# Four raw weight blocks, eight split pairs and two T2 tiles in place of 12 KB of DMA scratch

## The chip, the cores and the metric

The kernel runs on one NeuronCore of a Trainium2 chip. Its engines work side by side, each with a queue of its own: TensorE (PE; its weight loads are shown as PEld), VectorE (DVE), ScalarE (ACT), GpSimd (POOL) and SyncE (SP), which only issues DMAs. The metric is the device time of one execution in microseconds; the time of a kernel is the median of its runs.

## The reference

One layer of a bidirectional encoder on 1024 tokens of width 1024, in float32. Cut to what matters:

```python
x = x + 0.5 * rms_norm(swiglu(rms_norm(x, g1a), w1_in, w1_out), g1b)     # d_ff 2816
u = rms_norm(x, gma)
rq, rk, rv, rg, nq, nk, nv, g_ret, g_na = split(u @ w_mix_in)
y = bidirectional_retention(rotary(rq), rotary(rk) * 128 ** -0.5, rv)     # 4 heads, chunks of 128
y_ret = (silu(rg) * head_norm(y)) @ w_ret_out
y_na = neighbourhood_attention(nq, nk, nv, rel_bias) @ w_na_out           # 16 x 64 grid, 8 heads
x = x + rms_norm((sigmoid(g_ret) * y_ret + sigmoid(g_na) * y_na) @ w_out, gmb)
x = x + 0.5 * rms_norm(swiglu(rms_norm(x, g2a), w2_in, w2_out), g2b)
```

Every `@` is a matrix product of float32 numbers.

## The kernel before

A product of two float32 matrices is made of three matmuls. Each operand is split into a high part h (ScalarE rounds it to fp32r, L61) and a low part l (VectorE subtracts h from it, L62; in a few places GpSimd does), and TensorE adds up a_h·b_h, a_h·b_l and a_l·b_h in one bank (`mm3`, L88 to L90). So each block of weights that TensorE uses goes through a chain: a DMA from DRAM into a raw tile `wraw` of 128 x 1024 (`raw`, L70 to L73, issued by SyncE at L72), a cast and a subtraction for each half of 512 columns into a pair `wh`, `wl` (`piece`, L75 to L80), and then 12 or 24 matmuls. These tiles lie in one pool for the whole kernel, in rings: three of `wraw`, seven of `wh`, seven of `wl`. A load waits until a split has read the tile's last use; a split waits until TensorE has used the pair.

The two input products of the FFNs and most of the mix projection use Strassen's scheme in Winograd's form: seven products instead of eight. `Pairs.run` (L494 to L536) handles one pair of weight columns as a unit: it loads two raw blocks g and u (L498), and VectorE makes t1 = b12 - b11 (L510), t2 = b22 - t1 (L511), t3 = b22 - b12 (L521) and t4 = b21 - t2 (L530); t1, t3 and t4 overwrite the raw blocks, t2 has a tile of its own (L502), one for the kernel, called `t` in the profile. Each of them is split and multiplied (`product`), and VectorE adds the results up (L517 to L535). Two of VectorE's instructions, L510 and L521, are placed behind the result addition at L524 of the unit before (`behind`, L488). The first units of each such stage start early: their first two products are made ahead (`lead`, L454) and only the other five remain for `run`.

`ffn_in` runs 22 such units; its tile `gt`, one of three, takes the results (ScalarE's copy at L509 is the first write). `LeftFactors` (L562 to L607) makes operands of the output product from them and lets GpSimd store them to DRAM (`store`, L68), 14 stores of 256 KB for each two units. `ffn_out` (L674) reads them back block by block (L625). In its epilogue rows 4 to 7 of the residual come through `raw` (L699) as well, are added to the result (L659), stored (L660), normalised (L670) and transposed by TensorE (`flip`, L127), whereupon `Winograd.put` (L271 to L298) splits them and their sums. While this goes on, the first products of the mix stage, with weights loaded by `load_w` (L82), fill TensorE. The mix stage then runs 14 units of `Pairs`, the neighbourhood attention (`na_cores`, its K loaded as `kraw` at L879), the retention and the output products; `out_proj` (L104) takes weights by `load_w` and activations through `graw` (L850), both split in the same way, for three groups of token tiles.

What sets the order: each engine runs its queue in order, and the queues are fixed when the program is built. The Tile framework's planner takes the program's order as priority and dispatches, in a run that it simulates, what has its inputs and a free buffer; `high_priority`, `behind` and `issue_after` bend that. So the number of buffers enters twice: on the chip, where an instruction waits for a tile to come free, and when the queues are made. SyncE's queue carries the loads of `wraw` together with all others, so whatever stands behind a load that waits for a buffer waits too.

GpSimd issues its own DMAs in software, and the framework reserves a scratch for them in on-chip memory, 16 KB of each partition unless told otherwise. It is shared by all stores of `store`.

Of the kernel before, what the change touches and what calls it, by code (L numbers as in the profile page):

```python
# [10 lines left out]
F32 = mybir.dt.float32  # L11
F32R = mybir.dt.float32r
# [6 lines left out]
P = 128  # L19
D = 1024  # L20
# [18 lines left out]
class Core:  # L39
# [28 lines left out]
        self.nc.gpsimd.dma_start(dst, src)  # L68

    def raw(self, src, n=D):  # L70
        raw = self.wpool.tile([P, D], F32, tag="wraw", name="wraw", bufs=3)
        self.nc.sync.dma_start(raw[:, :n], src)  # L72
        return raw  # L73

    def piece(self, src, eng=None):  # L75

        h = self.wpool.tile([P, 512], F32R, tag="wh", name="wh", bufs=7)
        l = self.wpool.tile([P, 512], F32R, tag="wl", name="wl", bufs=7)
        self.split(h, l, src, eng=eng)
        return h, l  # L80

# [327 lines left out]
class Pairs:  # L409
# [84 lines left out]
    def run(self, i, out, done):  # L494

        c, nc = self.c, self.c.nc
        tt = nc.vector.tensor_tensor
        g, u = (c.raw(a) for a in self.srcs[i])  # L498
        b11, b21, b12, b22 = g[:, :512], g[:, 512:], u[:, :512], u[:, 512:]

        t1, t3, t4 = b11, b12, b21
        t2 = c.wpool.tile([P, 512], F32, tag="t2", name="t2", bufs=1)  # L502

        begun = self.begun.get(i)
        p1 = begun[0] if begun else self.product("a11", b11)
        c11, c12 = out(0), out(2)
        u1 = c12 if begun else c11
        for p, s in self.pieces(p1):
            nc.scalar.copy(u1[:, s], p)  # L509
        self.behind(tt(t1, b12, b11, ALU.subtract))  # L510
        tt(t2, b22, t1, ALU.subtract)  # L511
        p6 = self.product("s2", t2)
        if not begun:
            tt(c12, p6, c11, ALU.add)
        p2 = begun[1] if begun else self.product("a12", b21)
        for p, s in self.pieces(p2):
            tt(c11[:, s], p, u1[:, s], ALU.add)  # L517
        done(0)
        if begun:
            tt(c12, p6, c12, ALU.add)  # L520
        self.behind(tt(t3, b22, b12, ALU.subtract))  # L521
        p7 = self.product("s3", t3)
        c21 = out(1)
        self.last = tt(c21, p7, c12, ALU.add).ins  # L524
        p5 = self.product("s1", t1)
        c22 = out(3)
        tt(c22, p5, c21, ALU.add)
        tt(c12, p5, c12, ALU.add)
        done(3)
        tt(t4, b21, t2, ALU.subtract)  # L530
        p4 = self.product("a22", t4)
        tt(c21, p4, c21, ALU.add)
        done(1)
        p3 = self.product("s4", b22)
        self.end = tt(c12, p3, c12, ALU.add).ins  # L535
        done(2)  # L536
# [499 lines left out]
def ret_cores(c, pool, spool, d, dec, fill, n):  # L1036
# [12 lines left out]
    def split_qk(raw):  # L1049
        ops = {q: [pool.tile([P, S], F32R, tag=f"{q}{p}", name=f"{q}{p}", bufs=1) for p in "hl"] for q in "kq"}  # L1050
        for b in range(2):
            bs = slice(b * 512, (b + 1) * 512)
            for q in "kq":
                c.split(*[o[:, bs] for o in ops[q]], raw[q][:, bs])
        return ops
# [83 lines left out]
    for h in range(RH):  # L1139
# [4 lines left out]
        for cc in range(NC - 1, 0, -1):  # L1144
            update(h, 1, kb, cc, vget(cc), sb[:, cc] if cc < NC - 1 else None, sb[:, cc - 1])
            fill(n[2])
            if left and cc < NC - 1:
                store(*left.pop(0))
            if cc == NC - 2:
                ops = split_qk(raw)  # L1150
# [43 lines left out]
def trunk_layer(ctx: ExitStack, tc, x, xt, g1a, w1i, w1o, g1b, gma, wmt, wnv, wrv, logits, dtab, rope, bias,  # L1194
# [133 lines left out]
    with tc.tile_pool(name="pa", bufs=1, reuse_waits="tile") as pa:  # L1328
# [12 lines left out]
        for i, (_, _, f, g, fn) in enumerate(jobs):  # L1341
            parts = {}

            def part(j):
                parts[j] = half()
                return parts[j]

            def done(j):
                h = j % 2
                if fn == "rotary":  # L1350
                    rotate(turners[j], half(), parts[j], *tabs[h])
                elif fn is not None:
                    nc.scalar.activation(parts[j], parts[j], fn)
                c.store((f, g)[j // 2][:, h * 512:(h + 1) * 512], parts[j])
            mx.run(i, part, done)
            if i == 2:
                x1pool = pool(x1_stack, "x1b", "right")
                a21[:] = [x1pool.tile([P, 4, 512], F32R, name=f"a21{q}") for q in "hl"]
                for k in range(2):
                    raw = c.raw(d["a21"][:, 2 * k:2 * k + 2].rearrange("p k t -> p (k t)"))  # L1360
                    c.split(*[q[:, 2 * k:2 * k + 2].rearrange("p k t -> p (k t)") for q in a21], raw)
            if i == NHP - 1:
                for _ in vproj(wnv, ((4, 5, 6, 7),), done_nv):
                    pass
                for cb in range(4):
                    nc.sync.dma_start(d["nvg"][cb].rearrange("t (r c) d -> (t r) c d", r=4),
                                      d["nv"][:, KEY_OFF[cb]:KEY_OFF[cb] + 32, :])
# [216 lines left out]
```

## Time and profile before

| | |
|---|---|
| median of 3 runs | 2311.84 us (2311.79 to 2312.2) |
| the profiled execution | 2309.61 us, of which its span 2307.8 us |
| TensorE busy | 2215.0 us (96%), 10232 matmuls |
| VectorE busy | 1685.7 us (73%) |
| ScalarE busy | 1001.5 us (43%) |
| GpSimd busy | 647.0 us (28%) |
| mean granted clock of TensorE | 0.991 |
| moved by DMA | 444.11 MB, 192 GB/s over the span |
| loads of `wraw` from DRAM | 218 of 512 KB, 4.2 us from issue to landing (median) |

In a timeline row of the profile the columns are the start and the length in us, the engine ("SPq" is SyncE's queue, issuing a DMA), the line of the kernel, the operation, what it writes and reads, the shapes and how many like it follow each other; in square brackets stands how long the engine was idle before it, and what ended the wait. "A <- B: t, n, m" in the table of waits means that A waited for B for t us in all, n times, m us at most.

### The profile page before, as it was taken

How to read it: one execution, taken by the hardware profiler on the slowest of the kernel's cores; microseconds unless marked ns; L12 is line 12 of the kernel's file. 1: busy time of each engine (PE TensorE's matmuls, PEld its weight loads, DVE VectorE, ACT ScalarE, POOL GpSimd, SP SyncE). 2: the span in 40 equal slices, each digit the busy share in tenths (PEclk: the TensorE clock that was granted, in tenths of full speed). 3: DMA queues.
4: the chain of work that ended last, by engine and by line, in shares of the span. 5: the costliest groups of instructions: out<-in, count | busy, mean ns of one | idle time of the engine just before them, and what ended most of it. 6: DMA issues, size and time to landing. Idle time of an engine off the chain costs nothing.

```text
span 2307.8 us, 30216 instructions
## 1 busy us (share of the span) xinstructions
PE 2215.0 (96%) x10232; PEld 1828.7 (79%) x10232; DVE 1685.7 (73%) x2928; ACT 1001.5 (43%) x2086; POOL 647.0 (28%) x779
## 2 busy tenths in 40 slices
PE   7889999999998999999999999999799999999997
PEld 5678888888776877777888888787578888888886
DVE  7888888755558668869875678546999888885443
ACT  5433434332334222248885675315544343433232
POOL 1121212168424134411101222101431212215942
PEclk9999999999999999999999999999999999999999
DMA  6345434597545542357654466766534444349864
GB/s 237 132 143 181 169 132 174 184 381 291 202 150 173 178 164 96 109 189 234 219 177 153 164 224 228 281 210 206 168 137 163 159 159 167 141 151 367 304 232 164
DMA packets 150090, 444.11 MB, mean 192 GB/s; under 512 B 18800, under 2 KB 46576, under 8 KB 147824
## 3 DMA queue, kind: packets, MB, share of 16 engines
q1 hardware_dynamic: 111216, 314.23, 40.3%
q0 software_dynamic: 38720, 127.96, 14.4%
q8 instruction: 81, 1.33, 0.2%
q14 instruction: 73, 0.60, 0.1%
HBM read 305.80 MB, written 140.51 MB: 193 GB/s over the span
## 4 chain that ended last, share of the span: by engine, by line
PE 76%; DVE 11%; issue 5%; POOL 3%; DMA 3%; ACT 2%; SPq 0%; POOLq 0%; DVEq 0%; ACTq 0%
PE ps L90 23%; PE ps L88 23%; PE ps L89 23%; DVE wl L62 2%; PE pt L88 1%; PE pt L89 1%; PE pt L90 1%; DMA wraw<-in_dram 1%; PE pt L928 1%; POOL rstd L98 1%; PE ps L909 1%; DVE t L511 0%; ACT wh L61 0%; POOL cmb L294 0%; DVE wraw L521 0%
## 5 line engine op out<-in xcount | busy, mean ns | idle before, releaser
L62 DVE TENSOR_TENSOR wl<-wraw,wh 128x512 fp32r<-128x512 f32 x512 | 365.9, 732 | 81.7 <-ACT wh L61 80.5
L61 ACT CAST wh<-wraw 128x512 fp32r<-128x512 f32 x516 | 300.9, 618 | 219.1 <-DVE wraw L530 67.8
L89 PE MATMUL ps<-wl,g 128*128 128x512 f32 x484 | 188.7, 390 | 0.0
L90 PE MATMUL ps<-wh,g 128*128 128x512 f32 x484 | 188.4, 389 | 0.0
L88 PE MATMUL ps<-wh,g 128*128 128x512 f32 x484 | 188.3, 390 | 0.0
L552 ACT ACTIVATE c<-c 128x512 f32<-128x512 f32 x88 | 55.6, 632 | 209.6 <-DVE c L517 116.2
L62 DVE TENSOR_TENSOR wl<-w,wh 128x512 fp32r<-128x512 f32 x77 | 73.4, 966 | 89.5 <-ACT wh L61 87.2
L62 DVE TENSOR_TENSOR wl<-x,wh 128x512 fp32r<-128x512 f32 x77 | 77.8, 1025 | 83.1 <-ACT wh L61 82.4
L61 ACT CAST wh<-t 128x512 fp32r<-128x512 f32 x58 | 36.0, 621 | 182.1 <-DVE t L511 170.6
L88 PE MATMUL ps<-a11h,wh 128*128 128x512 f32 x276 | 110.2, 399 | 4.1 <-ACT wh L61 4.1
L88 PE MATMUL ps<-a22h,wh 128*128 128x512 f32 x280 | 109.8, 392 | 0.0
L90 PE MATMUL ps<-a12h,wl 128*128 128x512 f32 x276 | 108.0, 391 | 1.8 <-DVE wl L62 1.8
L88 PE MATMUL ps<-s2h,wh 128*128 128x512 f32 x232 | 93.2, 402 | 17.1 <-ACT wh L61 16.9
L89 PE MATMUL ps<-a22l,wh 128*128 128x512 f32 x280 | 109.1, 390 | 0.0
L90 PE MATMUL ps<-a22h,wl 128*128 128x512 f32 x280 | 109.1, 389 | 0.0
L89 PE MATMUL ps<-a11l,wh 128*128 128x512 f32 x276 | 108.8, 394 | 0.1
L88 PE MATMUL ps<-a12h,wh 128*128 128x512 f32 x276 | 108.8, 394 | 0.0
L90 PE MATMUL ps<-a11h,wl 128*128 128x512 f32 x276 | 108.4, 393 | 0.2
L89 PE MATMUL ps<-a12l,wh 128*128 128x512 f32 x276 | 107.6, 390 | 0.0
L89 PEld LDWEIGHTS ps<-wl,g 128*128 128x128 f32 x484 | 90.9, 188 | 19.5 <-DVE wl L62 1.0
L90 PEld LDWEIGHTS ps<-wh,g 128*128 128x128 f32 x484 | 90.9, 188 | 18.9
L88 PEld LDWEIGHTS ps<-wh,g 128*128 128x128 f32 x484 | 90.8, 188 | 18.9 <-ACT wh L61 0.2
(435 smaller groups left out, 6466.8 us busy)
## 6 DMA issues: line engine op xcount, KB each, us to landing
wraw<-in_dram SPq DMA_DIRECT2D x218, 512.0 KB, 4.2
g<-g0s SPq DMA_DIRECT2D x44, 512.0 KB, 4.3
g<-g1s SPq DMA_DIRECT2D x44, 512.0 KB, 4.7
g<-g0a SPq DMA_DIRECT2D x33, 512.0 KB, 3.3
g<-g1a SPq DMA_DIRECT2D x33, 512.0 KB, 4.7
g0s<-gth POOLq DMA_DIRECT2D x44, 256.0 KB, 5.3
g0s<-cmb POOLq DMA_DIRECT2D x44, 256.0 KB, 5.3
g1s<-gth POOLq DMA_DIRECT2D x44, 256.0 KB, 4.6
```

Of the source, the lines that this page charges most:

```text
L61: self.done = [nc.scalar.copy(h, src).ins, (eng or nc.vector).tensor_tensor(l, src, hf, ALU.subtract).ins]
L62: (eng or nc.vector).tensor_tensor(l, src, hf, ALU.subtract).ins]
L88: mm(ps, a[0], b[0], start=start, stop=False)
L89: mm(ps, a[0], b[1], start=False, stop=False)
L90: mm(ps, a[1], b[0], start=False, stop=stop)
L98: self.nc.gpsimd.tensor_tensor(r[:, :n], ms, self.mhalf[:, :n], ALU.pow)
L552: nc.scalar.activation(gate[j], gate[j], AF.Silu)
L909: nc.tensor.matmul(bv, q[:, rg * P:(rg + 1) * P], k, start=n == 0, stop=n == 1)
L928: nc.tensor.transpose(pt[:, j * P:(j + 1) * P], s[:, i % 2, (i // 2) * P:(i // 2 + 1) * P], c.ident)
```

## The change

The kernel is told to reserve 4 KB of each partition for GpSimd's DMAs, not 16. Of the 12 KB that come free the shared pool takes 10: a fourth `wraw` (4 KB), an eighth `wh` and an eighth `wl` (2 KB each), and a second `t2` (2 KB). No instruction is added or taken away.

```diff
     def raw(self, src, n=D):
-        raw = self.wpool.tile([P, D], F32, tag="wraw", name="wraw", bufs=3)
+        raw = self.wpool.tile([P, D], F32, tag="wraw", name="wraw", bufs=4)
         self.nc.sync.dma_start(raw[:, :n], src)
...
-        h = self.wpool.tile([P, 512], F32R, tag="wh", name="wh", bufs=7)
-        l = self.wpool.tile([P, 512], F32R, tag="wl", name="wl", bufs=7)
+        h = self.wpool.tile([P, 512], F32R, tag="wh", name="wh", bufs=8)
+        l = self.wpool.tile([P, 512], F32R, tag="wl", name="wl", bufs=8)
         self.split(h, l, src, eng=eng)
...
         t1, t3, t4 = b11, b12, b21
-        t2 = c.wpool.tile([P, 512], F32, tag="t2", name="t2", bufs=1)
+        t2 = c.wpool.tile([P, 512], F32, tag="t2", name="t2", bufs=2)
...
-    nc = _bacc.Bacc("TRN2", target_bir_lowering=False, num_devices=1)
+    nc = _bacc.Bacc("TRN2", target_bir_lowering=False, num_devices=1, dynamic_dma_scratch_size=4096)
```

## The prediction

> **What bounds the kernel now.** I read the page first (engines, then the forty slices), then who waits for whom on TensorE and on SyncE's queue, then the chain of waits, and last the timelines of the places where TensorE stands idle.
>
> ```profile
> span 2307.8 us, 30216 instructions
> PE 2215.0 (96%) x10232; PEld 1828.7 (79%) x10232; DVE 1685.7 (73%) x2928; ACT 1001.5 (43%) x2086; POOL 647.0 (28%) x779
> ...
> PE   7889999999998999999999999999799999999997
> ...
> DVE  7888888755558668869875678546999888885443
> ```
>
> TensorE is busy for 2215.0 of 2307.8 us, so every other engine together can give back 92.8 us at most. The slices show where: the first four, slices 11 to 18 (635 to 1039 us and around them), slices 28 to 30 (1.6 ms), and the last. The windows, whose columns are PE, PEld, DVE, ACT and POOL busy, the granted clock, the DMA share and GB/s, tell two kinds of stretch apart:
>
> ```profile
> 58.00:115.00 57.00, 47.35 (x199) 37.11 (x198) 49.95 (x82) 24.27 (x42) 8.28 (x15) 0.98 0.40 134
> ...
> 684.00:706.00 22.00, 14.56 (x59) 11.38 (x58) 18.59 (x34) 11.68 (x27) 7.49 (x10) 0.85 0.64 215
> ...
> 1630.00:1660.00 30.00, 23.40 (x83) 15.69 (x83) 27.07 (x35) 14.56 (x30) 15.31 (x12) 0.87 0.42 135
> ...
> 1731.00:2077.00 346.00, 346.00 (x1528) 286.44 (x1527) 288.78 (x468) 138.70 (x247) 68.19 (x127) 1.00 0.44 157
> ```
>
> From 1731 to 2077 TensorE is busy for all of 346 us at full clock: there no buffer can help. In the other three VectorE is busy for 84 to 90% and TensorE is not full: there the order of VectorE's queue and the arrival of its inputs decide. Now what TensorE waits for, and what SyncE's queue, ScalarE and VectorE wait for on the buffers that the change touches:
>
> ```profile
> PE ps L88 <- ACT wh L61: 22.5, 11, 5.9
> PE pt L342 <- POOL rstd L98: 12.2, 2, 11.0
> PE ps L89 <- DVE wl L62: 9.7, 6, 3.1
> PE ps L90 <- DVE wl L62: 9.2, 12, 2.0
> ...
> SPq L72 <- DVE wl L62: 1176.5, 176, 26.2
> ...
> ACT wh L61 <- PE ps L90: 143.3, 77, 6.3
> ...
> ACT wh L61 <- DMA wraw<-in_dram: 21.2, 12, 6.5
> ...
> DVE wraw L510 <- DMA wraw<-in_dram: 9.4, 7, 2.0
> ```
>
> SyncE's queue stands 1176.5 us in 176 waits at L72, the load of a raw block, until a split frees one of the three buffers; that alone costs nothing. It costs where the block then comes late: 21.2 + 9.4 = 30.6 us of ScalarE's and VectorE's time. TensorE itself waits 22.5 + 9.7 + 9.2 = 41.4 us for split blocks, the roof for the raw and split buffers together; the 12.2 us behind L98, at the start, are out of their reach. The 143.3 us that ScalarE waits for TensorE to free a wh are the sign of a full supply.
>
> **The change part by part.** It adds and removes no instruction; it moves loads and splits forward. All hangs on the places where TensorE stands idle.
>
> First two products (A), and the first change of unit (B):
>
> ```profile
> 37.70 0.50 PE L88 MATMUL ps<-a11h,wh 128*128 128x512 f32 x1 [1.77 <-ACT wh L61]
> ...
> 68.88 0.50 PE L90 MATMUL ps<-s1h,wl 128*128 128x512 f32 x1 [1.82 <-DVE wl L62]
> ...
> 79.19 0.50 PE L88 MATMUL ps<-s2h,wh 128*128 128x512 f32 x1 [2.27 <-ACT wh L61]
> ...
> 69.35 0.68 DVE L530 TENSOR_TENSOR wraw<-wraw,t 128x512 f32<-128x512 f32 x1
> ...
> 74.24 0.69 DVE L532 TENSOR_TENSOR c<-ps,c 128x512 f32<-128x512 f32 x1 [0.83 <-PE ps L90]
> ...
> 76.53 0.69 DVE L510 TENSOR_TENSOR wraw<-wraw 128x512 f32<-128x512 f32 x1 [1.60 <-DMA wraw<-in_dram]
> ...
> 71.44 2.32 SPq L72 DMA_DIRECT2D wraw<-in_dram  x2
> ```
>
> A: the idle 1.77 us can go with an earlier load, but TensorE then stands longer at 68.88, where VectorE, without a pause before it, sets the time (49.95 of 57 us busy, window above). I take 0; bounds 0 and 1.77. B: the load of 71.44 left when a split freed its buffer, and L510 waited 1.60 us for it; with a fourth buffer it has left before. I take 1.60; bounds 0 and the whole 2.27. **The second T2** is at 0: here the last reader of the first (L530, 69.35) is done more than 6 us before the next unit's L510, behind which L511 writes T2. Its cover is that L510 also waits for the unit before (behind, L488); without that L511 could move up by no more than B's 2.27, which is counted.
>
> The turn from the first FFN to the mix stage (C). Residual rows 4 to 7 come through the raw buffers too (L699), four rows for three buffers:
>
> ```profile
> 689.68 0.33 SPq L72 DMA_DIRECT2D wraw<-in_dram  x1
> ...
> 693.94 0.33 SPq L72 DMA_DIRECT2D wraw<-in_dram  x1
> ...
> 695.64 1.41 DVE L659 SCALAR_TENSOR_TENSOR wraw<-q,rstd,wraw 128x512 f32<-128x512 f32 x2 [1.77 <-DMA wraw<-in_dram]
> ...
> 699.12 1.20 PE L88 MATMUL ps<-wh,a12h 128*128 128x512 f32 x4 [1.44 <-ACT wh L61]
> 703.70 0.80 PE L89 MATMUL ps<-wl,a12h 128*128 128x512 f32 x1 [2.90 <-DVE wl L62]
> ```
>
> Row 7 is loaded at 689.68, when row 4 has left, and L659 waits 1.77 us for it; the weight block that TensorE needs at 699.12 goes behind it at 693.94. With four buffers row 7 is there and the weight takes its place, 4.26 us earlier. The 1.44 goes; of the 2.90, which end on VectorE's queue, the 1.77 of its own idle time go. I take 1.44 + 1.77 = 3.2; at least 1.77 (VectorE full otherwise), at most 1.44 + 2.90 and the slow first matmul after it (0.80 against 0.50 after the shorter stalls above), 4.6. A rule bears on this last term: by the Trainium skill, TensorE: Matmul & The Clock Gate, section "What's actually happening", the clock falls to half only after at least one idle window of about 3.4 us. By it a stall of 2.90 us has no such tail and the upper bound is 4.3; the 0.80 here says it can have one.
>
> Into the neighbourhood attention (D), and the out-projection (E):
>
> ```profile
> 1020.80 1.03 SPq L1127 DMA_DIRECT2D rg<-rg  x2
> 1024.05 0.34 SPq L72 DMA_DIRECT2D wraw<-in_dram  x1
> 1024.56 0.37 SPq L879 DMA_DIRECT2D kraw<-nk  x1
> ...
> 1035.39 0.44 PE L909 MATMUL ps<-k,qh 128*128 128x384 f32 x1 [3.14 <-DVE k L62]
> ...
> 1618.44 0.33 SPq L72 DMA_DIRECT2D wraw<-in_dram  x1
> ...
> 1623.19 0.62 ACT L61 CAST wh<-wraw 128x512 fp32r<-128x512 f32 x1 [1.84 <-DMA wraw<-in_dram]
> ...
> 1626.82 0.74 PE L89 MATMUL ps<-wl,gh 128*128 128x512 f32 x2 [3.05 <-DVE wl L62]
> ```
>
> D: queued behind L72 stand kraw, qraw, the bias and vraw. SyncE stood from 1021.83 to 1024.05 for a raw buffer, 2.22 us, and kraw left right after; TensorE then lost 3.14 us on K. kraw also needs room of the stage before, which this row doesn't show, so the gain is 0 to 2.22; I take half, 1.1. E: ScalarE waited 1.84 us for a block whose load waited for a buffer, and TensorE 3.05. I take 1.84; bounds 0 and 3.05, because VectorE is 27.07 of 30 us busy right after (window above). The eighth **wh and wl** let one more split, 0.62 us of ScalarE and 0.68 of VectorE, be done ahead there: inside these bounds. Elsewhere the supply is full and they are worth 0.
>
> **The scratch** serves the stores that GpSimd issues:
>
> ```profile
> L68 POOL DMA_DIRECT2D g0s<-cmb x44: 539/539/542, 103.7 to 480.9; - x44
> ...
> g0s<-cmb POOLq DMA_DIRECT2D x44, 256.0 KB, 5.3
> ...
> ACT gt L509 <- DMA g0a<-gt: 13.3, 2, 6.9
> ```
>
> Issue takes 539 ns each time and a store lands in 5.3 us, so about 5.3 / 0.54 = 10 can be under way. Whether a quarter of the scratch binds at 10 no row shows. Bounds: 0 (no store waits), and one landing more, 5.3 us, in each of the two bursts whose stores hold a gt buffer and so ScalarE (L509's two waits, 13.3 us): 10.6 lost. I take 0. By the Trainium skill, DMA: Bandwidth & Descriptors, sections "Terms" and "The descriptor swizzle", a descriptor has 16 B and a transfer over 128 partitions puts 9 per direction on each engine; 4096 B would then hold 256 of them, 28 such stores, an estimate above the 10.
>
> Sum: 0 + 1.60 + 3.2 + 1.1 + 1.84 = 7.7 us; all lower bounds 1.8, all upper 1.77 + 2.27 + 4.6 + 2.22 + 3.05 = 13.9. The profiled execution took 2309.6 us, 1.8 more than its span: it becomes 2301.9. The runs' median, 2311.84, lies 2.2 above it, so I forecast 2311.84 - 7.7 = 2304.
>
> **Rivals.** R1, the wait stays where it is: the blocks come earlier, but VectorE's queue holds its order, and only VectorE's idle time in C is won (1.8): 2310. For it: the stalls at 68.88, 703.70 and 1626.82 end on wl, not on a load; VectorE is 84 to 90% busy there. Against: L510, L659 and ScalarE's cast did stand idle for DMA. Loads moved forward may also meet the store bursts, with the like result.
>
> R2, slower: with an eighth pair free, the planner sets one more split ahead of the work that TensorE waits for. Place: VectorE's queue in the full stretches (58 to 231, 692 to 750, 1616 to 1700 us). Price: one wl, 0.68 us as the subtraction of the same size at 69.35, or up to 1.74 in the slow places:
>
> ```profile
> 849.24 3.47 DVE L62 TENSOR_TENSOR wl<-wraw,wh 128x512 fp32r<-128x512 f32 x2
> ```
>
> The three waits for split blocks count 11 + 6 + 12 = 29 stalls; if some 12 of them grow by 0.68 to 1.74 us the loss is 8 to 21, and with 1.8 us won the time is 2318 to 2331, at its likeliest 2319. It outweighs the 7.7 from 12 stalls of 0.68 or 5 of 1.74. For it: stalls that end on wl; against: splits stand behind older work by the program's order.
>
> R3, the change does less than it says because GpSimd waits for the scratch: 10.6 lost, 2311.84 - 7.7 + 10.6 = 2315.
>
> **How the numbers follow.** A measurement of this kernel can tell 0.2%, 4.6 us: faster means below 2307.2, slower above 2316.5. Forecast 0.53 (own range 2297 to 2307); R1 0.24; R2 0.19; R3 0.04. Of the forecast's and R1's spread a little crosses the line each way, and two in a hundred of R3: faster 0.55, same 0.25, slower 0.20. The range reaches from the upper bounds with a little spare (2296) into R2 (2319), which leaves out the costlier half of R2 and little below.
>
> **What will show it.** Right: L510 without its DMA wait at the first change of unit; row 7 loaded before any L659 of rows 4 to 7 and no 1.44 us idle after the flips; kraw issued without an L72 wait ahead; SyncE's 1176.5 us at L72 clearly fewer; issues on GpSimd still 539 ns. Wrong: the same waits with loads that land early (R1); more or longer TensorE waits on wl in the full stretches (R2); stores that start later than their data (R3); or an order so different that the five places no longer exist, which is what I can't see from here.

## The result

The changed kernel takes 2291.43 us (median of 4 runs, 2287.64 to 2294.17); the kernel before, run beside it, 2311.82. The ratio is 0.9918, with a 95% interval of 0.9901 to 0.9935: 20.4 us faster by the medians, where the prediction had 7.7. 2291.4 lies below the range that was given (2296 to 2319).

The profiled execution of the changed kernel took 2287.64 us, the shortest of its four, so its trace is some 4 us better than the median. Its page begins so (engines as before: busy time, share of the span, instructions):

```profile
span 2285.9 us, 30140 instructions
...
PE 2210.8 (97%) x10232; PEld 1828.4 (80%) x10232; DVE 1686.3 (74%) x2928; ACT 1000.7 (44%) x2086; POOL 650.9 (28%) x779
```

Every engine is about as busy as before; TensorE's 92.8 us of idle time have become 75.1. In the changed kernel's table of waits (us in all, times, longest) stand in the place of the rows shown before:

```profile
PE ps L88 <- ACT wh L61: 15.3, 7, 5.3
PE pt L342 <- POOL rstd L98: 13.4, 2, 11.3
PE ps L90 <- DVE wl L62: 10.4, 10, 4.9
PE ps L89 <- DVE wl L62: 4.8, 3, 3.0
...
SPq L72 <- DVE wl L62: 1109.3, 170, 30.1
...
ACT wh L61 <- DMA wraw<-in_dram: 23.3, 8, 6.5
...
ACT gt L509 <- DMA g0a<-gt: 10.1, 2, 6.9
```

TensorE's waits for split blocks fell from 41.4 to 30.5 us, though one of them, 4.9 us, is new. VectorE's L510 no longer waits for a load at all. But SyncE still stands 1109 us at L72 and ScalarE waits 23.3 us for raw blocks, 2 us more than before: not the picture of loads that simply come earlier.

Where the time changed is seen best by counting matmuls: all kernels here make the same 10232, and the table gives how much earlier (-) or later the k-th one starts than in the first profile of before, and in the last two columns the last matmul and the end of the span. All are read from the traces, one execution each; the columns are named by the time before.

| profile | 156 us | 635 | 783 | 877 | 901 | 1064 | 1377 | 1472 | 1744 | last | end |
|---|---|---|---|---|---|---|---|---|---|---|---|
| changed kernel | -7.8 | -7.9 | -15.6 | -17.4 | -11.5 | -13.9 | -12.3 | -15.6 | -18.9 | -18.9 | -22.0 |
| e9, before once more | -0.5 | -0.5 | -3.1 | -3.1 | -3.0 | -3.7 | -3.9 | -3.2 | -3.7 | -3.6 | -3.6 |
| e1, scratch alone | 0.3 | 0.4 | -1.2 | -1.3 | -1.2 | 0.0 | -0.2 | -2.3 | -2.7 | -2.7 | -5.8 |
| e7, scratch 8 KB | -1.9 | -1.9 | -1.6 | -1.6 | -1.6 | -0.8 | -1.0 | -4.7 | -4.2 | -4.2 | -7.3 |
| e2, all, old order | -0.5 | -1.0 | -4.2 | -4.3 | -4.2 | -8.0 | -7.7 | -9.8 | -12.4 | -12.4 | -15.5 |
| e3, raw | -6.3 | -6.4 | -8.0 | -9.7 | -3.8 | -4.6 | -3.7 | -3.8 | -2.2 | -2.3 | -5.3 |
| e4, pairs | -0.6 | -0.6 | -6.7 | -6.7 | -6.7 | -9.9 | -11.2 | -15.1 | -16.3 | -16.3 | -19.4 |
| e5, pairs, old order | -0.3 | -0.7 | -4.1 | -4.1 | -4.1 | -5.6 | -6.0 | -6.9 | -6.6 | -6.5 | -9.6 |
| e6, raw, old order | -0.8 | -0.8 | -3.3 | -3.3 | -3.3 | -6.3 | -6.5 | -10.0 | -12.9 | -12.9 | -16.0 |
| e8, two plans joined | -8.7 | -8.8 | -14.1 | -14.1 | -14.1 | -18.2 | -19.3 | -23.6 | -28.1 | -28.1 | -31.2 |
| e10, scratch 12 KB | 2.2 | 2.2 | 2.0 | 2.0 | 2.0 | 2.8 | 2.6 | 0.7 | -0.7 | -0.6 | -3.4 |
| e11, new order to 340 us | -8.4 | -9.0 | -13.4 | -13.4 | -13.4 | -16.6 | -17.0 | -19.2 | -21.4 | -21.4 | -24.5 |
| e12, one t2 | -7.6 | -7.7 | -13.6 | -15.4 | -9.0 | -12.3 | -12.4 | -15.0 | -17.3 | -17.3 | -20.4 |

Three things stand out in the first row that no term of the sum named: 8 us within the first FFN, a loss of 5.9 between 877 and 901 us, and 3.1 us gained behind the last matmul. (The 7.7 us between 635 and 783 lie where C does; e9 gains 2.6 there without any change.)

### The profile page after: what moved, and what is told of

It reads as the page before. It is cut to its first block, busy times and chain, and to the rows that moved or that the text cites. A ratio compares the mean times of both kernels' runs of the same rounds, so it can differ in the third digit from the quotient of the medians.

```text
span 2285.9 us, 30140 instructions
## 1 busy us (share of the span) xinstructions
PE 2210.8 (97%) x10232; PEld 1828.4 (80%) x10232; DVE 1686.3 (74%) x2928; ACT 1000.7 (44%) x2086; POOL 650.9 (28%) x779
## 5 line engine op out<-in xcount | busy, mean ns | idle before, releaser
L61 ACT CAST wh<-wraw 128x512 fp32r<-128x512 f32 x516 | 297.9, 618 | 213.5 <-DVE wraw L530 63.8
L61 ACT CAST wh<-t 128x512 fp32r<-128x512 f32 x58 | 36.0, 621 | 191.1 <-DVE t L511 191.0
L89 PEld LDWEIGHTS ps<-wl,g 128*128 128x128 f32 x484 | 90.9, 188 | 18.9 <-DVE wl L62 0.5
L90 PEld LDWEIGHTS ps<-wh,g 128*128 128x128 f32 x484 | 90.8, 188 | 18.9
L88 PEld LDWEIGHTS ps<-wh,g 128*128 128x128 f32 x484 | 90.8, 188 | 18.9
L68 POOL DMA_DIRECT2D g0a<-gth x33 | 18.0, 550 | 290.9 <-ACT gth L599 273.8
```

What stands on the lines that cost most here:

```text
L61: self.done = [nc.scalar.copy(h, src).ins, (eng or nc.vector).tensor_tensor(l, src, hf, ALU.subtract).ins]
L88: mm(ps, a[0], b[0], start=start, stop=False)
L89: mm(ps, a[0], b[1], start=False, stop=False)
L90: mm(ps, a[1], b[0], start=False, stop=stop)
```

## The experiments

Two theories were set against each other. **B** (buffers): the gain comes from loads and splits that wait less on the chip, as the prediction had it. **Q** (queues): the planner, which also reads the number of buffers, made other queues, and the gains and losses are theirs. The built programs bear on it: scratch alone, or scratch and the second t2, leave every queue as it was; the fourth raw buffer alone moves hundreds of rows from the lead of the first FFN on, the eighth pair alone moves TensorE's rows only from the end of that FFN on (VectorE's and ScalarE's already from 200 us).

### e1, e7, e10 and e9: the scratch

```diff
-    nc = _bacc.Bacc("TRN2", target_bir_lowering=False, num_devices=1)
+    nc = _bacc.Bacc("TRN2", target_bir_lowering=False, num_devices=1, dynamic_dma_scratch_size=4096)
```

e7 has 8192 there and e10 12288; e9 is the kernel before, unchanged.

> Only the scratch goes from 16 to 4 KB; the buffers stay 3, 7, 7 and 1, and every queue holds its order of before. Theory B (buffers: the gain comes from loads and splits that no longer wait on the chip) and theory Q (queues: it comes from the other order that the planner made of the queues, because it had more buffers): 2311.8, within 2 us, and the stores on GpSimd still issue in 539 ns and land in 5.3 us. Theory S (the scratch is itself part of it): slower, up to 2322, if stores wait for room; below 2307 if a smaller scratch helps.

> Scratch 8 KB and nothing else. In the traces GpSimd's drain at the end of the program takes 7.98 us with 16 KB and 2.92 with 4 KB, and only with 16 KB does it end behind the last store. Theory D (the drain is all that the scratch does): by a straight line it takes 4.6 us here, ends before the last store still, and the time is that with 4 KB, 2304. Theory S (the scratch also changes how the stores run): halfway or less, 2306 to 2308, with a time before the last matmul that differs.

> Scratch 12 KB and nothing else, to see GpSimd's drain at the end: 7.98 us with 16 KB, 2.68 with 8 and 2.92 with 4. If it goes with the size in steps, 8 us here; if by a line from 8 KB on, 5.3; if it depends on where in the scratch the last stores lie, anything from 2.5 to 8.

> The kernel before once more, for a second profile of the same program. Theory V (stalls vary from one execution to the next): TensorE's stalls between 684 and 735 us and at 1449 us come out some us shorter or longer, so that the 2 to 4 us by which e1 and e7 differ from the first profile there are no effect of the scratch. Theory S (they are an effect of the scratch): the stalls come out as in the first profile, to 0.3 us. By both GpSimd's drain at the end takes 8 us.

e1: 2304.29 us against 2309.48, ratio 0.9975 (0.9964 to 0.9986). e7: 2304.59 against 2309.01, 0.9982 (0.9971 to 0.9992). e10, one run: 2306.23; e9, one run: 2305.98, beside runs of before from 2303.02 to 2310.41. The scratch alone is thus worth 4 to 5 us, and I had it at 0. The larger part lies at the end of the program, in an instruction that is counted as busy nowhere: GpSimd's drain. The view of line 1580 (the end of the program) gives its shortest, median and longest duration in ns and when the first and the last begin; the loads and stores that SyncE issues are from the timeline. Before, with 16 KB:

```profile
L1580 POOLq DRAIN  x3: 40/93/7984, 2299.1 to 2307.6; - x3
...
2291.60 10.24 SPq L660 DMA_DIRECT2D out_dram<-w  x8
```

The changed kernel, with 4 KB:

```profile
L1580 POOLq DRAIN  x3: 40/93/2922, 2280.2 to 2285.6; - x3
...
2272.72 10.26 SPq L660 DMA_DIRECT2D out_dram<-w  x8
```

e10 with 12 KB, and e7 with 8 KB:

```profile
L1580 POOLq DRAIN  x3: 40/102/5207, 2298.4 to 2304.2; - x3
```

```profile
L1580 POOLq DRAIN  x3: 40/93/2677, 2294.9 to 2300.3; - x3
```

With 16 KB the drain begins at 2299.1 and lasts 7.98 us, to 2307.1; the last output store was issued at 2301.8 and the span ends at 2307.8, 6.0 us later. With 4 KB it lasts 2.92 us, and from the last store's issue (2283.0) to the end (2285.9) it is 2.9 us. So 3.1 us go, and the end is then set by the last store; the remaining 2 us by which the drain is shorter are hidden. 12 KB and 8 KB (5.21 and 2.68 us) lie on a line with 16, some 0.65 us for each KB; 4 KB does not go on along it, and the straight line that I had expected of 8 KB (4.6) was wrong, though its time came out as forecast. e9 has 7.99 us again.

e9 also shows how far one execution of the same program differs from another: 3.6 us at the last matmul, most of it between 684 and 760 us. So the differences there in e1 and e7, up to 2.1 us, need no effect of the scratch to explain them (theory V). One stall does go with it: at 1449 us TensorE waits 2.2 us for ScalarE in both profiles with 16 KB and 0.2 to 0.3 us in the three with less. With the 3.1 us at the end that makes about e1's 5.2. Why this stall goes was not tried and stays open.

### e2, e5 and e6: the buffers without the new queues

The kernel is built twice. The first build, with the buffers of before, gives the order of each engine's queue; in the second, with more buffers, each instruction gets an edge to the one before it in that order (an order of issue, not a wait), so that the planner can only repeat it. In the traces every queue of e2, e5 and e6 has the order of before, but for two small VectorE rows at 1022 us in e2 and e6. Shortened:

```diff
+    nc, feeds, names, _ = build(dict(raw=3, wh=7, wl=7, t2=1))
+    order = [i.name for bb in nc.main_func.blocks for i in bb.instructions if i.name in set(names)]
+    nc, feeds, _, _ = build(dict(raw=4, wh=8, wl=8, t2=2), order)      # e5: 3, 8, 8, 1; e6: 4, 7, 7, 1
...
+        for n in order:                                                # in the second build
+            i = by[n]
+            if i.engine in last:
+                tc.add_manual_dep(i, last[i.engine], mybir.DependencyInfo(
+                    mybir.DependencyClass.NoSync, mybir.DependencyReason.DATA), reason="order")
+            last[i.engine] = n
```

> All four parts of the change, but every engine's queue is held in its order of before: the kernel plans once with 3, 7, 7 and 1 buffers, and then again with 4, 8, 8 and 2 and the first plan's order. Only what the buffers do on the chip is left. Theory B: the whole gain, 2291, with the 5.94 us idle of TensorE at 141 us gone. Theory Q: what my prediction's five places give at most, 2304, and as little as 2310, with the 5.94 us still there.

> Queues held in their order of before, as in e2, with the scratch and the eighth wh and wl alone (3 raw, 1 t2). e2 was 2293 and the scratch alone 2304. Theory R (raw, as the prediction had it: the 11 us between them are L510, kraw and the out-projection no longer waiting for a raw buffer): 2304 here, and TensorE's 3.14 us idle on K is as long as before. Theory W (pairs: splits done earlier free the raw blocks earlier too): 2294, with the idle on K 0 to 1.

> The same order with the scratch and the fourth raw buffer alone (7 wh, 7 wl, 1 t2). Theory R: 2294, and the 2.27 us idle at the first change of unit and the 3.14 on K are gone. Theory W: 2302 to 2304, at most the first of the two stalls is gone.

e2: 2293.34, ratio 0.9932 (0.9920 to 0.9944). e5: 2301.68, 0.9972 (0.9961 to 0.9984). e6: 2292.95, 0.9937 (0.9923 to 0.9951). With the queues held, the fourth raw buffer is worth 11.3 us beside the scratch (e6 against e1) and the eighth pair nothing that can be measured (e5 against e1). Of the two theories about the parts, R holds; of B and Q neither alone: 2293 is nearer to B's 2291 than to Q's 2304, but the 5.94 us stall at 141 us is still there in e2 (6.6 us), as Q had said. The places of the prediction, in the timeline of e6:

```profile
74.74 0.68 DVE L510 TENSOR_TENSOR wraw<-wraw 128x512 f32<-128x512 f32 x1
77.58 0.50 PE L88 MATMUL ps<-s2h,wh 128*128 128x512 f32 x1 [0.77 <-ACT wh L61]
...
693.39 1.41 DVE L659 SCALAR_TENSOR_TENSOR wraw<-q,rstd,wraw 128x512 f32<-128x512 f32 x2
...
701.43 0.51 PE L89 MATMUL ps<-wl,a12h 128*128 128x512 f32 x1 [2.75 <-DVE wl L62]
...
1012.06 0.90 SPq L1127 DMA_DIRECT2D rg<-rg  x2
1015.65 0.34 SPq L72 DMA_DIRECT2D wraw<-in_dram  x1
1016.16 0.33 SPq L879 DMA_DIRECT2D kraw<-nk  x1
1029.09 0.45 PE L909 MATMUL ps<-k,qh 128*128 128x384 f32 x1
...
1615.99 0.74 PE L89 MATMUL ps<-wl,gh 128*128 128x512 f32 x2 [3.57 <-DVE wl L62]
```

B: L510 has no wait left and TensorE's 2.27 us have become 0.77. C: L659 no longer waits for row 7 and the 1.44 us are gone, but the 2.90 are still 2.75, on VectorE. D: kraw is issued at 1016.2, where e1 issues it at 1023.8, and TensorE no longer waits for K; the L72 just ahead of it still waits, from 1012.96 to 1015.65. E: its stall, 3.05 us, is now 3.57.

### e3, e4 and e12: the parts with the planner's own queues

```diff
-        raw = self.wpool.tile([P, D], F32, tag="wraw", name="wraw", bufs=3)
+        raw = self.wpool.tile([P, D], F32, tag="wraw", name="wraw", bufs=4)      # e3
-        h = self.wpool.tile([P, 512], F32R, tag="wh", name="wh", bufs=7)
-        l = self.wpool.tile([P, 512], F32R, tag="wl", name="wl", bufs=7)
+        h = self.wpool.tile([P, 512], F32R, tag="wh", name="wh", bufs=8)         # e4
+        l = self.wpool.tile([P, 512], F32R, tag="wl", name="wl", bufs=8)         # e4
```

All have the scratch of 4 KB; e12 has both edits, and one t2.

> The scratch and the fourth raw buffer alone; the queues take another order from the lead of the first FFN on. Theory B: the prediction put all of the gain at the raw buffer, so 2291. Theory Q: what the new order gives in the first FFN and at its end, by the two traces 8 + 6 us less and some losses later, 2300; and the 4.89 us idle at 865 us is there or not, according to which buffer moved the rotary units.

> The scratch and the eighth wh and wl alone; the queues differ from those of before only from the end of the first FFN on. Theory B: 2311, since TensorE's supply was full. Theory Q: some us to either side, 2306 to 2318, since the order moves without the blocks coming earlier; the rival R2 of the prediction (a split put ahead of urgent work) shows here as 2318, with new waits on wl at 865 and 1350 us.

> The change without the second t2; the planner then moves eight rows of VectorE's and ScalarE's queues. By the prediction the second t2 is worth 0: 2291, as the changed kernel. If it is what lets L511 go ahead of L554: 2296 to 2299, with a stall of some us at 141.

e3: 2304.04, ratio 0.9974 (0.9964 to 0.9985). e4: 2290.21, 0.9920 (0.9908 to 0.9932). e12: 2290.62, 0.9926 (0.9913 to 0.9939). The parts have changed places: the raw buffer, worth 11 us with the old queues, is worth nothing (e1 had 2304.29) with the queues that the planner makes for it, and the pair, worth nothing, is worth 14. The same buffers, two orders, some 11 us each way (e6 to e3, and e5 to e4): that is Q. e4, without the fourth raw buffer, is as fast as the changed kernel. The second t2 is worth nothing, as forecast. Whether e4's order would gain as much with only seven pairs was not tried and stays open. Nor was its gain traced to single waits: against e5 it comes in steps, 2.6 us by 783 us, 4.3 by 1064, 5.2 by 1377, 8.2 by 1472 and 9.7 by 1744.

What the new order of the raw buffer does is seen at two places. First the gain at 141 us, which e3, e12 and the changed kernel have and e4 does not (in the table, the column of 156 us). Before:

```profile
136.28 0.54 POOL L68 DMA_DIRECT2D g0a<-gt  x1 [1.14 <-DVE gt L600]
143.63 0.58 ACT L509 COPY gt<-pt 128x512 f32<-128x512 f32 x1 [6.94 <-DMA g0a<-gt]
...
144.78 0.69 DVE L554 TENSOR_TENSOR gt<-c,gt 128x512 f32<-128x512 f32 x1 [3.80 <-ACT c L552]
145.99 0.68 DVE L511 TENSOR_TENSOR t<-wraw 128x512 f32<-128x512 f32 x1
146.76 0.62 ACT L61 CAST wh<-t 128x512 fp32r<-128x512 f32 x1 [0.64 <-DVE t L511]
147.43 0.80 PE L88 MATMUL ps<-s2h,wh 128*128 128x512 f32 x1 [5.94 <-ACT wh L61]
```

The changed kernel:

```profile
135.66 0.54 POOL L68 DMA_DIRECT2D g0a<-gt  x1 [0.73 <-DVE gt L600]
139.80 0.69 DVE L511 TENSOR_TENSOR t<-wraw 128x512 f32<-128x512 f32 x1
140.26 0.59 ACT L509 COPY gt<-pt 128x512 f32<-128x512 f32 x1 [3.23 <-DMA g0a<-gt]
...
141.27 0.61 ACT L61 CAST wh<-t 128x512 fp32r<-128x512 f32 x1
141.41 0.69 DVE L554 TENSOR_TENSOR gt<-c,gt 128x512 f32<-128x512 f32 x1 [0.32 <-ACT c L552]
141.94 0.50 PE L88 MATMUL ps<-s2h,wh 128*128 128x512 f32 x1
```

GpSimd's stores stand in another order, the one that L509 waits for lands 3.4 us earlier, and VectorE's L511, which needs nothing of it, is ahead of L554 and no longer behind it: from L509 to the matmul it is 1.7 us, not 3.8. Both are orders of queues: e2 has the same buffers in the order of before, and there the stall stays.

Then the loss in the rotary units, also of e3, e12 and the changed kernel, VectorE's queue in the latter:

```profile
859.85 0.69 DVE L527 TENSOR_TENSOR ev<-ps,ev 128x512 f32<-128x512 f32 x1 [2.03 <-PE ps L90]
...
861.15 0.69 DVE L1030 TENSOR_TENSOR ev<-ev,tab 64x512 f32<-64x512 f32 x1
...
867.23 1.64 DVE L1033 TENSOR_TENSOR ev<-ev 128x512 f32<-128x512 f32 x1
868.79 1.75 DVE L62 TENSOR_TENSOR wl<-wraw,wh 128x512 fp32r<-128x512 f32 x1
...
870.60 0.80 PE L90 MATMUL ps<-a11h,wl 128*128 128x512 f32 x1 [4.89 <-DVE wl L62]
```

The cast of that block (L61) was done at 851.6, VectorE stood idle three times for 2 us after that, and yet its subtraction stands behind the eight operations of the rotary embedding (L1030 to L1033, twice), some 6 us. TensorE waits 4.89 us for it.

### e11 and e8: two plans joined

Both have all four parts and queues held as in e2, but from two plans, joined at about 340 us, where both plans have issued the same instructions: up to there the order that 4, 8, 8 and 2 buffers gave, from there in e11 that of before (3, 7, 7, 1) and in e8 that of 3, 8, 8 and 2, which is e4's. Shortened:

```diff
+    names, first = planned(dict(raw=4, wh=8, wl=8, t2=2))
+    _, second = planned(dict(raw=3, wh=7, wl=7, t2=1))      # e8: 3, 8, 8, 2
...
+            order += first[e][:cut] + second[e][cut:]       # for each engine e
...
+    nc, feeds, _, _ = build(dict(raw=4, wh=8, wl=8, t2=2), order)
```

> All four parts; the queues in the changed kernel's order up to about 340 us and in the order of before from there on. e2, wholly in the order of before, was 2293.3. Theory Q (the new order of the first FFN ends the second stall of its store bursts, 5.94 us, by VectorE's L511 ahead of L554): 2293.3 less 7.5, 2286. Theory B: 2293, since the buffers are the same as in e2.

> All four parts of the change; the queues are held in two plans joined at about 340 us: up to there the order that 4, 8, 8 and 2 buffers gave (the changed kernel's), from there the order that 3, 8, 8 and 2 gave (that of e4). Theory Q (gains and losses sit in the order: -7.8 us in the first FFN with the one, no 4.89 us idle in the rotary units with the other): 2290.2 less 7.5, 2283, faster than both. Theory B (they sit in the buffers on the chip): as the changed kernel, 2291.

e11: 2283.91, ratio 0.9895 (0.9878 to 0.9911). e8: 2280.89, 0.9880 (0.9864 to 0.9896). The buffers are those of e2 and of the changed kernel; only the queues differ. The front's new order is worth 9.4 us by the medians (e2 to e11), 7.9 in the traces by 156 us. Behind it the changed kernel's own order costs 7.5 us by the medians against that of before (e11 to the changed kernel) and 10.5 against e4's (e8 to the changed kernel). These kernels ran in different sets, and against the kernel before in each set the losses are 3.7 and 7.7; e12, in e11's set and with the changed kernel's order but for a few rows, is 6.7 slower than e11. The sign is sure (every run of e11 is shorter than every run of the changed kernel and of e12), the size is not. e8 is the fastest kernel here, 1.2% faster than before and faster than the changed kernel.

## Why the prediction was wrong

By the medians the 20.4 us add up as follows: 5.2 scratch (e1 against its before), 11.0 buffers on the chip (e1 to e2), 9.4 new order in the first FFN (e2 to e11), 7.5 given back by the new order after it (e11 to the changed kernel): 18.1; the other 2.3 are the difference between the medians of before in two sets of runs (2311.82 and 2309.48). With each kernel taken against the before of its own set, the gain in the first FFN is 7.9 and the loss after it 3.7, and the sum is 20.4. Each has an uncertainty of some 3 to 5 us.

- **"It moves loads and splits forward"** is the step that failed. The sum took the queues as given. The prediction named the other case last ("an order so different that the five places no longer exist") and gave it no price; R2 had it in part. It is worth a gain of 8 to 9 us and a loss of 4 to 7 here: either is about as large as the whole forecast, and that they partly cancel is chance.
- **The scratch at 0, bounds 0 to 10.6 lost** failed by its sign: no gain was allowed for. Its reasoning on the stores was right: with 4 KB the issues take 542 ns, against 539, and nothing shows a store waiting, so the estimate of 28 stores by the Trainium skill (DMA: Bandwidth & Descriptors) is not contradicted. No run tries its limit, and the Trainium skill counts its 9 descriptors for a transfer of 1 MiB, where these stores have 256 KB. The gain is at a place that the prediction left out, the end of the program (3.1 us), and in the stall at 1449 us (2). The trace of before showed the first: from the last store's issue to the end of the span 6 us pass.
- **The sum of A to E, 7.7**, answers to what e2 and e6 measure with the old queues, 11. That the gain is the raw buffer's was right, and so was 0 for the pair and for the second t2, as long as the queues hold. That 7.7 lies near 11 is partly luck, since the terms miss both ways. By terms, e6 against e1, e7 and e9:
  - A, 0: right (1.77 us as before).
  - B, 1.60: 1.5 us of TensorE's 2.27 went, and by 156 us 0.8 were left, no more than e9 and e7 show without the buffer (0.5 and 1.9).
  - C, 3.2: both waits went, the 1.44 on the weight block and VectorE's 1.77 on row 7, but they don't add up. TensorE's next stall ends on VectorE's queue, which is ahead by as much, so the matmul after the 2.90 comes 2.3 us earlier, 0.8 of them brought along; and in the table e6 gains no more by 783 us than e9.
  - D, 1.1, bounds 0 to 2.22: the stall went whole, 3.1 us, and by the table e6 gains 3.0 from 783 to 1064 us where e1, e7 and e9 lie between 1.2 lost and 0.6 gained. kraw left 7.6 us earlier than in e1 (2 of them are e6's lead by then), not 2.22: I had priced only the last L72 ahead of it, and that wait is still there (2.7 us); it is the loads before it that moved up.
  - E, 1.84: its stall stayed and the stretch from 1472 to 1744 us still gained 2.9, against 0.4 in e1. Smaller stalls that the sum left out went there instead: 0.95 us at 1604, and 1.10, 0.96 and 0.87 between 1648 and 1653, all in before and none in e6; against that, 1.50, 0.46 and 0.46 from 1635 on became one of 3.98 at 1627.
- **The slow matmul after C's stall**, 0.3 us in the upper bound, was mis-sized. In the trace of before not one matmul is slow but fourteen, for 6.0 us. Such matmuls start every 0.23 us at full clock, so fourteen would take 3.2 us, and 2.8 are lost. In e9 the slow stretch at this place lasts 3.5 us, in e1 there is none: a part of what one execution differs from another between 684 and 760 us. The columns are those of the windows in the prediction, the granted clock third from the end:

```profile
703.70:709.70 6.00, 6.00 (x14) 4.70 (x15) 6.00 (x9) 2.87 (x6) 3.22 (x2) 0.51 0.48 163
709.70:715.70 6.00, 6.00 (x32) 4.97 (x31) 5.28 (x8) 4.33 (x9) 1.60 (x2) 1.00 0.12 18
```

- **R1** (VectorE's queue holds its order) is what happened in C and E. **R2** did happen, once and with another cause: a split put behind work that could wait, 4.89 us at 865 us, made by the raw buffer's plan (e3, e12 and the changed kernel). The eighth pair, to which R2 gave the blame, has no such stall (e4). **R3**: nothing for it.
- **What was to show it**: L510 without its wait and row 7 in time: yes. kraw without an L72 wait ahead: no, in e6 as above; in the changed kernel TensorE still loses 2.5 us at its place, then on the split of q. SyncE's time at L72 "clearly fewer": 1109.3 of 1176.5, little; the likely reason, not tested, is that the one more buffer is filled at once and the queue then waits for the next to come free. "Issues on GpSimd still 539 ns": 542.

## What to carry to other kernels

Where a planner makes the queues from the number of buffers, a buffer is two changes; hold the queues' order fixed to price the buffer, and then compare plans piece by piece, since the best order of one stretch can be joined to that of another. A load behind a chain of waiting loads can move up by more than the wait just ahead of it, since the whole chain moves. Waits on one path don't add up: when two go, look where the next one on that path ends. Look at what follows the last matmul: an engine that is idle may still have a drain to do.

## What was not expected of the hardware

GpSimd's drain at the end takes 7.98, 5.21, 2.68 and 2.92 us with 16, 12, 8 and 4 KB of scratch; why 4 KB isn't below 8 stays open.

After a stall TensorE's matmuls of 128x512 take 0.5 us and then 0.4, or some 0.8 and then 0.63 for a while. In the fourteen traces every stall of 3.57 us or more that ends on such a product is followed by slow ones, at once or within 1.6 us. Of the shorter stalls some are and some are not: the 3.14 us of before ahead of K (there a product of 128x384) have none, but a stall of 2.46 us in e9 has them at once:

```profile
702.41 0.74 PE L89 MATMUL ps<-wl,a12h 128*128 128x512 f32 x1 [2.46 <-DVE wl L62]
```

After the 3.57 us of e6, shown above, four matmuls run first, and the granted clock (third from the end) falls about 1 us behind the end of the stall:

```profile
1616.00:1617.00 1.00, 1.00 (x4) 0.85 (x5) 1.00 (x4) 0.68 (x3) 0.23 (x1) 1.00 0.24 94
1617.00:1619.60 2.60, 2.60 (x7) 1.88 (x6) 2.52 (x4) 0.62 (x1) 0.56 (x1) 0.50 0.66 216
```

The Trainium skill, TensorE: Matmul & The Clock Gate, section "What's actually happening", has the clock fall after at least one idle window of about 3.4 us that runs freely. That all stalls of 3.57 us or more are followed by slow matmuls agrees with it; that one of 2.46 us can be doesn't, and here the measurement decides.
